# Forgetting attention: the reciprocal and scaling of a head behind the next head's minimum, and query, sample and memory steps held to places between the heads

## The chip, the cores and the metric

The kernel runs on 1 core of one Trainium2 chip. The metric is the device time of one execution in microseconds (us), the median over runs; lower is better. Engines are named as in the profile: PE is the matrix engine (PEld its weight loads), DVE the vector engine, ACT the scalar engine, POOL the general-purpose engine, SP the engine that issues most DMAs.

## The reference, cut to what matters

One inference step of a two-layer decoder trunk for a prompt of 512 tokens and 8 samples of 4 new tokens each, model width 1024. Layer 0 mixes state-space heads with sliding-window attention, layer 1 is the forgetting attention; each layer then has cross-attention into 256 memory tokens and a gated feed-forward network. The change lies in layer 1's mixer:

```python
def fox_attend(q, k, v, cum, q_off):
    '''Queries sit at key indices q_off..q_off+Tq-1; logit[t,s] += cum[t]-cum[s].'''
    ...
    bias = cq[..., :, None] - c[..., None, :]
    mask = jnp.arange(tk)[None, :] <= (q_off + jnp.arange(tq))[:, None]
    return gqa_attend(q, k, v, mask=mask, bias=bias)     # softmax(q k / 8 + bias) v

def fox_prompt(q, k, v, logf):                            # 4 blocks of 128 queries
    cum = jnp.cumsum(logf, axis=1)
    ...
    o = lax.map(lambda a: fox_attend(a[0], k, v, cum, a[1]), (qb, offs))

def mem_kv(mem, g, wk, wv):                               # the memory's keys and values, per layer
    mn = rms_norm(mem, g)
    return (mn @ wk)..., (mn @ wv)...
```

There are 16 query heads of 64 on 4 key heads. The samples attend in the same way to 1024 cached keys each, read page by page (128 keys a page) through a page table, and to their own 4 new ones.

## The kernel before

Everything is kept transposed: 128 features on the partitions, tokens along the free dimension. A float32 product is made of three faster ones, from a high and a low part of each factor, so each weight piece is loaded by SP, cast on ACT (L162) and its rest taken on DVE (L163) before PE uses it; `linear_steps` then yields after each output tile of 24 matmuls (8 of 128 inputs, three parts).

The order of work is settled when the program is built. Instructions are written in program order; a planner then fixes each engine's own order by estimated costs, taking among what is ready by its estimate that which was written first. So a piece of work written later can be planned ahead of a waiting one. `after` adds an edge that the planner obeys and that costs no wait on the chip. Tiles in the small accumulator memory (PSUM) have a tag each, and `psum` gives how many of a tag may be live: "tr" 3 (linear tiles), "sc" 2 (scores), "tp" 2 (transposes), "pv" 1 (values).

The forgetting attention (`odd`, from L1067) works on the prompt in 8 blocks, two halves `m` of the key heads by four blocks `c` of 128 queries, and each block has 8 heads (`fox_prompt`), 64 heads in all. A head of block `c` has W = 128 (c + 1) keys:

1. two score matmuls of W columns on PE (high part of the keys, then low part) into an "sc" tile (`bank`, L125);
2. on DVE the sum of scores and mask, its negative, and the smallest of that, in one instruction (L1183);
3. on ACT the exponential and the sum of it (L1184);
4. on DVE the reciprocal of the sum (L1185), and on POOL the scaling by it (L1186);
5. two heads later (`FOX_AHEAD`) `turn`: c + 1 transposes on PE (L141), copied by ACT or DVE in turn (L1166); after the block's last head the product with the values, copied out on DVE (L1173).

At the start of a block `fox_queries` (L1136) builds the block's high and low queries, 6 instructions on ACT and DVE. Between the heads the loop takes steps from three generators at the heads that `FOX_PLAN` (L40) lists: "q", the second half of the query projection (8 tiles); "s", the samples (`fox_sample`, L1243), in four groups of two samples, each with scores, softmax, transposes, and values, and with the loads of the next group's pages (32 DMAs of 128 KB on SP, L1260, keys then values); "m", the keys and values of layer 1's memory (`mem_begin`, `mem_k`, `mem_v`). Nothing but the planner's estimates keeps a step at its place.

After the loop the remaining heads are turned, the generators run out, the attention's output is split into parts (L246, L249) and multiplied by the output weights (`wo_d`), whose loads are held behind the copy of block 5's values (`whold`).

Of the kernel before, what the change touches and what calls it, by code (L numbers as in the profile page):

```python
# [14 lines left out]
AF = mybir.ActivationFunctionType  # L15
# [91 lines left out]
class Net:  # L107
    def __init__(self, nc, tc, ctx, I, O):
        self.nc, self.tc, self.ctx, self.I, self.O = nc, tc, ctx, I, O
        self.n = self.turn = 0  # L110
        self.hold = self.whold = self.last = None
# [25 lines left out]
    def mm(self, out, lhsT, rhs, start, stop):  # L137
        self.nc.tensor.matmul(out, lhsT, rhs, start=start, stop=stop)  # L138

    def tr(self, out, in_, k=P):  # L140
        self.nc.tensor.transpose(out, in_, self.ident[0:k, 0:k])  # L141
# [869 lines left out]
    def odd(self, st, nxt, fill):  # L1011
        nc, tc, I, O = self.nc, self.tc, self.I, self.O
        with ExitStack() as es:
# [53 lines left out]
            with tc.tile_pool(name="fox", bufs=1) as fx:  # L1067
                self.pvs = []
# [12 lines left out]
                self.banks = ['sc']  # L1081
# [28 lines left out]
    def fox_keys(self, kT, ncum):  # L1110
# [21 lines left out]
        self.zero(mask[:, 0:384])  # L1132
        self.after(nc.gpsimd.tensor_copy(mask[:, 384:512], self.cst[:, C_SWA + 128:C_SWA + 256]), self.last)
# [15 lines left out]
    def fox_prompt(self, q, K2, V, m, c, ahead):  # L1149
# [4 lines left out]
        Q = self.fox_queries(q, m, tok)  # L1154
# [19 lines left out]
        for r in range(2):  # L1174
            for i in range(4):
                sc = self.bank([P, 512])
                for z in range(2):
                    self.mm(sc[:, 0:W], Q[z][:, r, i], K2[z][:, m, r, 0:W], z == 0, z == 1)
# [6 lines left out]
                nc.vector.reciprocal(rec, den)  # L1185
                nc.gpsimd.tensor_scalar(pr[:, 0:W], pr[:, 0:W], rec, 1.0, ALU.mult, ALU.mult)  # L1186
                ahead.append((turn, pr, r, i))
                self.fox_turn(ahead, FOX_AHEAD)
                yield

# [52 lines left out]
    def fox_sample(self, q, kTs, Qb, ncs, V, lf, fx, S, sel):  # L1243
# [25 lines left out]
        self.sample_q(q, Qb)  # L1269
        for G in range(4):  # L1270
            sc = [self.psum("sc", [P, 4, 128]), self.psum("sc", [P, 4, 128])]
            sn = self.psum("tp", [P, 32])
            for u in range(2):
                self.mm(sc[u].rearrange("p a b -> p (a b)"), sel[:, 128 * (G % 2):128 * (G % 2) + 128], S[:, G // 2, 512 * u:512 * u + 512], True, False)
                for b2 in range(2):
                    for m in range(2):
                        a = 64 * b2 + 32 * m
                        lq = Qb[:, 2 * G + b2, m].rearrange("p r i t -> p (r i t)")
                        self.mm(sc[u][a:a + 32], lq, keys[G, b2][:, 4 * u:4 * u + 4, 128 * m:128 * m + 128], False, True)
# [7 lines left out]
            wk = self.prt[:, 2560:4736]  # L1287
            pr = wk[:, 0:1056]
# [4 lines left out]
            mx, nm, den, d1, rec = self.ty(3), self.ty(1), self.ty(3), self.ty(1), self.ty(1)  # L1293
            for u in range(2):
                nc.vector.tensor_reduce(mx[:, u:u + 1], sc[u].rearrange("p a b -> p (a b)"), AX.X, ALU.max)
            nc.vector.tensor_reduce(mx[:, 2:3], pr[:, 1024:1056], AX.X, ALU.max)
            nc.vector.tensor_reduce(nm, mx, AX.X, ALU.max, negate=True)
            for u in range(2):
                nc.scalar.activation(pr[:, 512 * u:512 * u + 512], sc[u].rearrange("p a b -> p (a b)"), AF.Exp, bias=nm, accum_out=den[:, u:u + 1])
            nc.scalar.activation(pr[:, 1024:1056], pr[:, 1024:1056], AF.Exp, bias=nm, accum_out=den[:, 2:3])  # L1300
            nc.vector.tensor_reduce(d1, den, AX.X, ALU.add)
            nc.vector.reciprocal(rec, d1)
# [17 lines left out]
            self.sample_o(q, Osb, G, 1)  # L1320
            if G < 3:
                load(vals, G + 1, "fox_v")
            yield


    def mem_begin(self, l):
# [12 lines left out]
        for k in range(KD):  # L1339
            g = self.par[:, G_MEM + 8 * l + k:G_MEM + 8 * l + k + 1]  # L1340
            self.split(mh, ml, raw[:, k], k, 0, 256, g)
            if first:
                self.square_acc(acc, raw[:, k], k, 256)
        if first:
            self.rstd(acc, self.mcol, self.mb, [(0, 0, 128), (1, 128, 128)])
# [381 lines left out]
    def run(self):  # L1727
# [5 lines left out]
        def memory(l):  # L1733
# [3 lines left out]
            m = self.mem_begin(l)  # L1737
# [129 lines left out]
```

## Time and profile before

| | |
|---|---|
| time, median of 3 runs | 1679.29 us (1678.39 to 1679.85) |
| the profiled execution's own time | 1679.51 us |
| its span in the profile | 1677.7 us |
| granted PE clock over the span | 0.993 |
| busy, share of the span | PE 97%, PEld 91%, DVE 71%, ACT 47%, POOL 20% |
| the fox stage's heads | 64, their minima from 992.9 us to 1157.8 us |

A row of a group reads: line, engine, operation, output<-inputs by the program's names, shape, count, then busy us, mean ns of one, then idle us of the engine just before them and what ended it. A row of the timeline reads: start in us, us taken, engine, line, operation, and in brackets the engine's idle time before it and what ended that. A row of a wait reads: who <- whom: us in total, times, longest. An SP row is the time to issue the DMAs, not to move the bytes. Matmuls are pipelined: a row's length is longer than the distance to the next.

### The profile page before, as it was taken

To read this page: it belongs to the slowest core of one execution; us is meant where nothing else is said; L and a number is where in the kernel's file an instruction comes from. 1 tells how busy PE (TensorE), PEld (TensorE's weight loads), DVE (VectorE), ACT (ScalarE), POOL (GpSimd) and SP (SyncE) were. 2 spreads that over 40 slices of the span, in tenths; PEclk is the share of its full clock that TensorE was granted. 3 is DMA by queue.
4 is the path that set the end of the run, shared out by engine and by line. 5 is a ranking of instruction groups with operands and counts; after the bars stand their busy time and mean duration, and the time that the engine had idled before them with its cause. 6 is when DMAs were issued, how large, how long until landed. Compare 5 with 4: busy or idle time off the path is not lost.

```text
span 1677.7 us, 32465 instructions
## 1 busy us (share of the span) xinstructions
PE 1627.3 (97%) x12720; PEld 1518.5 (91%) x12720; DVE 1196.5 (71%) x2322; ACT 795.1 (47%) x1637; POOL 333.5 (20%) x510
## 2 busy tenths in 40 slices
PE   6999999999999999999999998998999999999997
PEld 6999999868998999999999995656989999999997
DVE  6678789777777876767667577654667876767753
ACT  4367645344545444444445255544545444444434
POOL 6022323675422200000002103111313100000002
PEclk9999999999999999999999999999999999999999
DMA  5121243156442232323224433555451232323222
GB/s 187 55 64 52 86 154 126 37 192 217 156 138 91 94 113 83 107 77 114 82 70 135 141 118 110 165 170 186 132 183 52 86 125 85 109 86 102 76 72 83
DMA packets 71221, 189.27 MB, mean 113 GB/s; under 512 B 7612, under 2 KB 34012, under 8 KB 63452
## 3 DMA queue, kind: packets, MB, share of 16 engines
q1 hardware_dynamic: 69388, 184.84, 33.3%
q8 instruction: 100, 1.64, 0.4%
q10 hardware_dynamic: 1600, 1.83, 0.4%
q0 software_dynamic: 80, 0.52, 0.1%
q14 instruction: 53, 0.43, 0.1%
HBM read 172.22 MB, written 14.95 MB: 112 GB/s over the span
## 4 chain that ended last, share of the span: by engine, by line
PE 89%; DVE 4%; POOL 2%; issue 1%; DMA 1%; ACT 1%; DVEq 0%; SPq 0%; POOLq 0%; ACTq 0%
PE ps L138 64%; PE ps L1586 22%; PE ps L141 3%; POOL room L425 1%; DMA vr<-wd_v 0%; ACT prt L1184 0%; DMA o_s_ssm<-hb 0%; DVE meml L252 0%; DMA room<-wo_d 0%; DVE xs L902 0%; ACT split_t L162 0%; POOL sq L421 0%; DVE split_t L1567 0%; POOL E L862 0%; DVE prt L1183 0%
## 5 line engine op out<-in xcount | busy, mean ns | idle before, releaser
L138 PE MATMUL ps<-xh,split_t 128*128 128x288 f32 (+1 forms) x2304 | 463.9, 293 | 13.8 <-ACT split_t L162 11.8
L138 PEld LDWEIGHTS ps<-xh,split_t 128*128 128x128 f32 x2304 | 370.7, 190 | 17.0 <-ACT split_t L162 12.7
L1586 PE MATMUL ps<-xf,split_t 128*128 128x272 f32 x2592 | 348.9, 289 | 3.1 <-DVE split_t L1567 2.2
L138 PE MATMUL ps<-xl,split_t 128*128 128x256 f32 (+1 forms) x1152 | 338.5, 295 | 1.2 <-DVE xl L252 1.0
L1586 PEld LDWEIGHTS ps<-xf,split_t 128*128 128x128 f32 x2592 | 335.0, 188 | 4.4 <-DVE split_t L1567 3.1
L261 POOL TENSOR_TENSOR room<-room,sq 128x256 f32<-128x256 f32 (+1 forms) x96 | 87.4, 914 | 768.9 <-ACT sq L260 767.3
L138 PEld LDWEIGHTS ps<-xl,split_t 128*128 128x128 f32 x1152 | 218.5, 190 | 4.1 <-DVE xl L252 2.3
L138 PE MATMUL ps<-hh,fs 128*128 128x256 f32 (+1 forms) x1024 | 206.3, 288 | 0.0
L162 ACT CAST split_t<-room 128x1024 fp32r<-128x1024 f32 (+1 forms) x128 | 130.2, 1019 | 154.5 <-PE ps L138 112.2
L163 DVE TENSOR_TENSOR split_t<-room,split_t 128x1024 fp32r<-128x1024 f32 (+1 forms) x128 | 157.3, 1231 | 35.7 <-ACT split_t L162 35.1
L138 PEld LDWEIGHTS ps<-hh,fs 128*128 128x128 f32 x1024 | 164.9, 188 | 0.4 <-ACT fs L1630 0.4
L1567 DVE TENSOR_TENSOR split_t<-fr,split_t 128x1024 fp32r<-128x1024 f32 x108 | 131.7, 1220 | 36.6 <-ACT split_t L1566 36.4
L1566 ACT CAST split_t<-fr 128x1024 fp32r<-128x1024 f32 x108 | 113.4, 1052 | 90.5 <-PE ps L1586 54.7
L138 PE MATMUL ps<-hl,fs 128*128 128x256 f32 (+1 forms) x512 | 147.3, 288 | 0.0
L138 PE MATMUL ps<-oh,split_t 128*128 128x288 f32 (+1 forms) x512 | 107.2, 298 | 1.2 <-ACT oh L246 1.2
L138 PEld LDWEIGHTS ps<-hl,fs 128*128 128x128 f32 x512 | 96.4, 188 | 0.0
L138 PEld LDWEIGHTS ps<-oh,split_t 128*128 128x128 f32 x512 | 83.5, 192 | 6.1 <-ACT oh L246 3.0
L1630 ACT CAST fs<-room 128x512 fp32r<-128x512 f32 x64 | 39.4, 618 | 81.3 <-PE ps L138 67.2
L138 PE MATMUL ps<-ol,split_t 128*128 128x288 f32 (+1 forms) x256 | 76.1, 297 | 0.3 <-DVE ol L249 0.2
L252 DVE SCALAR_TENSOR_TENSOR xl<-x,room,xh 128x256 fp32r<-128x256 f32 (+1 forms) x96 | 69.7, 756 | 5.5 <-ACT xh L251 5.4
L138 PE MATMUL ps<-hh,split_t 128*128 128x256 f32 (+1 forms) x384 | 73.4, 288 | 0.0
L1643 DVE TENSOR_TENSOR x<-x,ps 128x256 f32<-128x256 f32 (+1 forms) x128 | 54.3, 433 | 25.7 <-PE ps L138 25.4
(426 smaller groups left out, 3118.7 us busy)
## 6 DMA issues: line engine op xcount, KB each, us to landing
fr<-wfi SPq DMA_DIRECT2D x36, 1024.0 KB
room<-wfo SPq DMA_DIRECT2D x64, 256.0 KB
room<-wo_e SPq DMA_DIRECT2D x16, 512.0 KB
xk<-mem_k SPq DMA_DIRECT2D x8, 1024.0 KB
xv<-mem_v SPq DMA_DIRECT2D x8, 1024.0 KB
room<-wfi SPq DMA_DIRECT2D x16, 512.0 KB
fox_k<-fox_k SPq DMA_DIRECT2D x64, 128.0 KB
fox_v<-fox_v SPq DMA_DIRECT2D x64, 128.0 KB
```

Of the source, the lines that this page charges most:

```text
L138: self.nc.tensor.matmul(out, lhsT, rhs, start=start, stop=stop)
L141: self.nc.tensor.transpose(out, in_, self.ident[0:k, 0:k])
L162: nc.scalar.copy(hi[:, 0:n], raw[:, 0:n])
L163: nc.vector.tensor_tensor(lo[:, 0:n], raw[:, 0:n], hi[:, 0:n].bitcast(F32), ALU.subtract)
L252: return nc.vector.scalar_tensor_tensor(ll, src, g, hh.bitcast(F32), ALU.mult, ALU.subtract)
L261: nc.gpsimd.tensor_tensor(acc, acc, sq[:, 0:N], ALU.add)
L425: nc.gpsimd.tensor_tensor(acc, acc, sq, ALU.add)
L1566: nc.scalar.copy(hi, t)
L1567: nc.vector.tensor_tensor(lo, t, hi.bitcast(F32), ALU.subtract)
L1586: self.nc.tensor.matmul(ps, w[a][:, k], x[:, b, k], start=start and k == 0 and i == 0, stop=k == 3 and i == 2, skip_group_check=True)
L1630: nc.scalar.copy(hi, raw)
L1643: nc.vector.tensor_tensor(x, x, ps, ALU.add)
```

## The change

It makes five edits, all in the fox stage but one.

- The reciprocal and the scaling of a head (`fox_scale`) are written after the next head's minimum and exponential; the last one after the loop.
- `mm` and `tr` give their instruction back, and `placed` sets an edge (`after`) from the first matmul or transpose of each step to the second score matmul of the head (`scored`) after which the step stands. The planner may no longer move a step's PE work ahead of that head. `FOX_PLAN` has other places: the query steps at heads 2 to 24, the samples' 17 steps at 25 to 58, the memory's 10 at 19 to 60, and two memory steps between the turns of the last heads.
- The next block's queries are built at the block's fourth head.
- A sample group takes its two score tiles one after the other, each finished by the minimum instruction (against a tile of zeros) that also copies it out; one exponential of 1056 columns takes the place of three; the group's last transpose and copies (`sample_o`) move behind the next yield. `mem_begin` of layer 1 yields after every second slice.
- The counts of "tr" and "sc" tiles become 4 and 3, in the whole kernel, and heads use two "sc" and one "tr" tile in turn from the start.

```diff
-for _a, _heads in (("q", range(4, 33, 4)), ("s", [33,34,36,38,40,41,43,45,47,49,51,53,55,57,59,61]), ("m", range(34, 64, 4))):
+for _a, _heads in (("q", (2, 4, 7, 10, 13, 16, 20, 24)), ("s", (25, 26, 28, 31, 33, 34, 36, 40, 41, 42, 44, 47, 49, 50, 52, 56, 58)), ("m", (19, 21, 23, 25, 35, 37, 39, 46, 54, 60))):
...
-        bufs = {"tr": 3, "sc": 2, "tp": 2, "pv": 1}[tag]
+        bufs = {"tr": 4, "sc": 3, "tp": 2, "pv": 1}[tag]
...
-        self.nc.tensor.matmul(out, lhsT, rhs, start=start, stop=stop)
+        return self.placed(self.nc.tensor.matmul(out, lhsT, rhs, start=start, stop=stop))
...
+    def placed(self, i):
+        if self.behind is not None:
+            self.behind, d = None, self.behind
+            self.after(i, d)
+        return i
...
-                self.banks = ['sc']
+                self.banks = ['sc', 'sc', 'tr']
...
-                for m in range(2):
-                    for c in range(4):
-                        for _ in self.fox_prompt(q, K2, V, m, c, ahead):
-                            heads += 1
-                            self.banks = ['sc'] if heads < 33 else ['sc', 'sc', 'tr']
-                            for a in FOX_PLAN.get(heads, ""):
-                                next(gens[a], None)
-                self.fox_turn(ahead, 0)
+                blocks = [(m, c) for m in range(2) for c in range(4)]
+                ready = lambda m, c: self.fox_queries(q, m, slice(128 * c, 128 * c + 128))
+                Q = ready(*blocks[0])
+                for j, (m, c) in enumerate(blocks):
+                    for _ in self.fox_prompt(Q, q, K2, V, m, c, ahead):
+                        heads += 1
+                        if heads % 8 == 4 and j < 7:
+                            nq = ready(*blocks[j + 1])
+                        for a in FOX_PLAN.get(heads, ""):
+                            self.behind = self.scored
+                            next(gens[a], None)
+                        self.behind = None
+                    Q = nq
+                self.fox_scale()
+                for _ in range(FOX_AHEAD):
+                    next(gens["m"], None)
+                    self.fox_turn(ahead, len(ahead) - 1)
...
-                nc.vector.reciprocal(rec, den)
-                nc.gpsimd.tensor_scalar(pr[:, 0:W], pr[:, 0:W], rec, 1.0, ALU.mult, ALU.mult)
+                self.fox_scale()
+                self.unscaled = pr[:, 0:W], rec, den
                 ahead.append((turn, pr, r, i))
                 self.fox_turn(ahead, FOX_AHEAD)
                 yield
+
+    def fox_scale(self):
+        if self.unscaled:
+            pr, rec, den = self.unscaled
+            self.nc.vector.reciprocal(rec, den)
+            self.nc.gpsimd.tensor_scalar(pr, pr, rec, 1.0, ALU.mult, ALU.mult)
+            self.unscaled = None
...
         for G in range(4):
-            sc = [self.psum("sc", [P, 4, 128]), self.psum("sc", [P, 4, 128])]
...
             for u in range(2):
+                sc = self.bank([P, 4, 128])
...
+                nc.vector.tensor_tensor_reduce(pr[:, 512 * u:512 * u + 512], sf, self.zeros.to_broadcast([P, 512]), -1.0, 1e30, ALU.add, ALU.min, mx[:, u:u + 1])
+                if u == 0:
+                    yield
...
-            gate = nc.vector.tensor_tensor(pr[:, 1024:1056], sn, c[:, C_MN + 32 * G:C_MN + 32 * G + 32], ALU.add)
+            gate = nc.vector.tensor_tensor_reduce(pr[:, 1024:1056], sn, c[:, C_MN + 32 * G:C_MN + 32 * G + 32], -1.0, 1e30, ALU.add, ALU.min, mx[:, 2:3])
             if G < 3:
                 load(keys, G + 1, "fox_k")
-            yield
-            ...
-            for u in range(2):
-                nc.scalar.activation(pr[:, 512 * u:512 * u + 512], sc[u].rearrange("p a b -> p (a b)"), AF.Exp, bias=nm, accum_out=den[:, u:u + 1])
-            nc.scalar.activation(pr[:, 1024:1056], pr[:, 1024:1056], AF.Exp, bias=nm, accum_out=den[:, 2:3])
+            nc.vector.tensor_reduce(nm, mx, AX.X, ALU.min)
+            nc.scalar.activation(pr, pr, AF.Exp, bias=nm, scale=-1.0, accum_out=den)
...
-            self.sample_o(q, Osb, G, 1)
             if G < 3:
                 load(vals, G + 1, "fox_v")
             yield
+            self.sample_o(q, Osb, G, 1)
```

More of the change, by code (lines that the diff above doesn't have):

```diff
@@ L110, in __init__ @@
         self.n = self.turn = 0
-        self.hold = self.whold = self.last = None
+        self.hold = self.whold = self.last = self.behind = None
         pool = lambda name, **k: ctx.enter_context(tc.tile_pool(name=name, bufs=1, **k))
@@ L1132, in fox_keys @@
         self.zero(mask[:, 0:384])
+        self.zeros = mask[:, 0:1]
         self.after(nc.gpsimd.tensor_copy(mask[:, 384:512], self.cst[:, C_SWA + 128:C_SWA + 256]), self.last)
@@ L1147, in fox_queries, with fox_prompt @@
         return Q
-    def fox_prompt(self, q, K2, V, m, c, ahead):
+    def fox_prompt(self, Q, q, K2, V, m, c, ahead):
         nc = self.nc
@@ L1269, in fox_sample @@
         self.sample_q(q, Qb)
+        yield
         for G in range(4):
-            sc = [self.psum("sc", [P, 4, 128]), self.psum("sc", [P, 4, 128])]
             sn = self.psum("tp", [P, 32])
+            wk = self.prt[:, 2560:4736]
+            pr = wk[:, 0:1056]
+            mx = self.ty(3)
             for u in range(2):
-                self.mm(sc[u].rearrange("p a b -> p (a b)"), sel[:, 128 * (G % 2):128 * (G % 2) + 128], S[:, G // 2, 512 * u:512 * u + 512], True, False)
+                sc = self.bank([P, 4, 128])
+                sf = sc.rearrange("p a b -> p (a b)")
+                self.mm(sf, sel[:, 128 * (G % 2):128 * (G % 2) + 128], S[:, G // 2, 512 * u:512 * u + 512], True, False)
                 for b2 in range(2):
@@ L1278, in fox_sample @@
                         lq = Qb[:, 2 * G + b2, m].rearrange("p r i t -> p (r i t)")
-                        self.mm(sc[u][a:a + 32], lq, keys[G, b2][:, 4 * u:4 * u + 4, 128 * m:128 * m + 128], False, True)
+                        self.mm(sc[a:a + 32], lq, keys[G, b2][:, 4 * u:4 * u + 4, 128 * m:128 * m + 128], False, True)
+                nc.vector.tensor_tensor_reduce(pr[:, 512 * u:512 * u + 512], sf, self.zeros.to_broadcast([P, 512]), -1.0, 1e30, ALU.add, ALU.min, mx[:, u:u + 1])
+                if u == 0:
+                    yield
             for b2 in range(2):
@@ L1286, in fox_sample @@
                 self.mm(sn[a:a + 64], ncs.rearrange("p h t -> p (h t)"), self.ident[0:32, 0:32], False, True)
-            wk = self.prt[:, 2560:4736]
-            pr = wk[:, 0:1056]
-            gate = nc.vector.tensor_tensor(pr[:, 1024:1056], sn, c[:, C_MN + 32 * G:C_MN + 32 * G + 32], ALU.add)
+            gate = nc.vector.tensor_tensor_reduce(pr[:, 1024:1056], sn, c[:, C_MN + 32 * G:C_MN + 32 * G + 32], -1.0, 1e30, ALU.add, ALU.min, mx[:, 2:3])
             if G < 3:
                 load(keys, G + 1, "fox_k")
-            yield
-            mx, nm, den, d1, rec = self.ty(3), self.ty(1), self.ty(3), self.ty(1), self.ty(1)
-            for u in range(2):
[L1295 to L1299, printed above, removed]
-            nc.scalar.activation(pr[:, 1024:1056], pr[:, 1024:1056], AF.Exp, bias=nm, accum_out=den[:, 2:3])
-            nc.vector.tensor_reduce(d1, den, AX.X, ALU.add)
-            nc.vector.reciprocal(rec, d1)
+            nm, den, rec = self.ty(1), self.ty(1), self.ty(1)
+            nc.vector.tensor_reduce(nm, mx, AX.X, ALU.min)
+            nc.scalar.activation(pr, pr, AF.Exp, bias=nm, scale=-1.0, accum_out=den)
+            nc.vector.reciprocal(rec, den)
             yield
@@ L1343, in mem_begin @@
                 self.square_acc(acc, raw[:, k], k, 256)
+            elif k % 2:
+                yield
         if first:
@@ L1736, in memory @@
             nc.gpsimd.memset(t[:, 0:1], 0.0)
-            m = self.mem_begin(l)
+            m = yield from self.mem_begin(l)
             yield from self.mem_k(l, m, self.mk)
```

7 lines of the change are left out of this document (3 added, 4 removed).

## The prediction

> **What bounds the kernel now.** I read the page first (engines, forty slices), then stretches of the fox stage, then its groups by shape, its waits and its timeline.
>
> ```profile
> span 1677.7 us, 32465 instructions
> PE 1627.3 (97%) x12720; PEld 1518.5 (91%) x12720; DVE 1196.5 (71%) x2322; ACT 795.1 (47%) x1637; POOL 333.5 (20%) x510
> PEld 6999999868998999999999995656989999999997
> ```
>
> The matrix engine is the bound, but a matmul's row is longer than the time it keeps the next one waiting, so PE at 97% hides losses. The weight loads (PEld) show them: slices 25 to 28, 42 us each, fall to 5 or 6 tenths. That is the forgetting attention, 990 to 1165 us, the one stage that this change edits. Stretches of it, and a dense one after it (stretch, length, then busy us and count of PE, PEld, DVE, ACT, POOL, then granted clock, DMA share, GB/s):
>
> ```profile
> 990.00:995.00 5.00, 5.00 (x43) 5.00 (x42) 4.15 (x12) 1.73 (x5) 0.38 (x1) 1.00 0.30 78
> 1000.00:1005.00 5.00, 5.00 (x43) 4.81 (x43) 4.55 (x16) 3.43 (x10) 1.13 (x4) 1.00 0.62 187
> 1030.00:1035.00 5.00, 4.25 (x20) 2.27 (x18) 3.67 (x14) 3.72 (x11) 1.77 (x3) 1.00 0.02 3
> 1100.00:1105.00 5.00, 5.00 (x21) 2.79 (x21) 0.55 (x1) 0.37 (x1) 0.00 (x0) 1.00 0.65 192
> 1145.00:1150.00 5.00, 1.37 (x14) 0.80 (x7) 0.92 (x1) 1.99 (x5) 0.22 (x1) 0.81 0.62 233
> 1150.00:1155.00 5.00, 4.38 (x20) 4.15 (x21) 4.88 (x19) 3.55 (x11) 1.39 (x2) 0.51 0.38 108
> 1175.00:1180.00 5.00, 5.00 (x42) 5.00 (x41) 4.66 (x8) 3.63 (x9) 2.51 (x3) 1.00 0.87 357
> 990.00:1047.00 57.00, 52.07 (x325) 39.33 (x323) 43.95 (x146) 32.57 (x92) 17.23 (x36) 1.00 0.45 139
> 1047.00:1165.00 118.00, 109.38 (x880) 72.43 (x879) 66.99 (x225) 59.19 (x164) 19.03 (x35) 0.97 0.52 154
> ```
>
> A dense stretch does 42 matmuls of 256 or 288 columns in 5 us, 0.119 us each, or 21 of 512 columns, 0.238 each. While query projections ran beside the heads (990, 1000) PE did 43 in 5 us. At 1030, with the projections used up, it did 20, mostly small. The stage's PE work, priced so, from groups of 990 to 1165 (shapes, count, busy us, mean ns) and from runs of back-to-back rows:
>
> ```profile
> L141 PE MATMUL ps<-room,prt 128*128 128x128 f32 x192 | 32.8, 280 | 2.4 <-POOL prt L1186 0.9 <-DVE q L582 0.4 <-ACT prt L1299 0.4
> L138 PE MATMUL ps<-PT,odd 128*64 128x512 f32 x72 | 25.5, 608 | 0.5 <-ACT PT L1166 0.5
> L138 PE MATMUL ps<-fox_k,odd 128*32 128x512 f32 x64 | 13.5, 604 | 0.0
> L138 PE MATMUL ps<-fox_v,prt 128*32 128x128 f32 x256 | 9.0, 275 | 0.0
> L138 PE MATMUL ps<-split_t,memh 128*128 128x512 f32 x32 | 10.9, 402 | 0.5 <-ACT prt L1311 0.5
> L138 PE MATMUL ps<-split_t,meml 128*128 128x512 f32 x16 | 6.3, 393 | 0.0
> L138 PE MATMUL ps<-kh,qst 128*128 128x512 f32 x16 | 7.8, 488 | 2.2 <-DVE ty L1183 2.2
> L138 PE MATMUL ps<-kl,qst 128*128 128x512 f32 x16 | 6.3, 395 | 0.0
> ...
> 1042.28 0.44 PE ps L141 x4
> ...
> 1038.10 1.94 PE L138 MATMUL ps<-PT,odd 128*64 128x512 f32 x8
> ...
> 1142.60 1.74 PE L138 MATMUL ps<-fox_v,prt 128*32 128x128 f32 x56
> ```
>
> Transposes 192 x 0.11 (0.44 for four) = 21; probabilities times values 72 x 0.24 (1.94 for eight) = 17.5; cached keys 13.5 by their busy time; cached values 256 x 0.031 (1.74 for 56) = 8; 80 of 512 columns x 0.238 = 19; the other 541 of the 1205 (325 and 880 above), mostly of 256 and 288 columns, x 0.119 = 64. Sum 143 us of the stage's 175: **32 us are lost**. DVE's 111 us (43.95 and 66.99) fit beside that, and ACT's 92. Where the loss sits, first a head of 384 keys, then the waits that end in it (weight loads, then DVE):
>
> ```profile
> 1028.71 0.54 DVE L1183 CUSTOM_DVE_ANT_0 prt<-ps,prt 128x384 f32<-128x384 f32 x1
> ...
> 1029.29 0.62 ACT L1184 ACTIVATE prt<-prt,ty 128x384 f32<-128x384 f32 x1 [0.69 <-DVE ty L1183]
> 1029.81 0.18 ACT L1184 ACTIVATION_READ_ACCUMULATOR prt<-prt,ty 128x1 f32 x1
> ...
> 1030.03 0.16 DVE L1185 RECIPROCAL ty<-ty 128x1 f32<-128x1 f32 x1 [0.24 <-ACT prt L1184]
> 1030.11 0.54 DVE L1183 CUSTOM_DVE_ANT_0 prt<-ps,prt 128x384 f32<-128x384 f32 x1
> ...
> PEld ps L138 <- DVE ty L1183: 9.8, 16, 0.9
> ...
> L1185 DVE RECIPROCAL ty<-ty 128x1 f32<-128x1 f32 x64 | 10.3, 161 | 20.2 <-ACT prt L1184 19.5
> ...
> ACT split_t L162 <- DMA room<-wo_d: 3.8, 1, 3.8
> ...
> 1141.80 0.85 SPq L158 DMA_DIRECT2D room<-wo_d  x2
> ```
>
> The minimum (L1183), the exponential (L1184) and the reciprocal (L1185) make a ring: DVE runs in order, so the next minimum waits behind a reciprocal that waits for ACT. 1028.71 to 1030.11 is 1.40 us a head, of which DVE works 0.78. The last two rows are the end: an output weight asked for at 1141.80 is late, its cast stands at the head of ACT's queue with a head's exponential behind it, and PE drops to 1.37 of 5 us.
>
> **The change part by part.**
>
> *Reciprocal and scaling behind the next minimum.* No instruction more or less. Removed from the ring: ACT's 0.62 + 0.18 and two hand-overs; DVE then does the next minimum in that time. The gain is bounded by the 20.2 us that DVE idled before L1185 and by 0. I take 8: nearest is the 9.8 us that PE's weight loads stood behind L1183, less a little, because the next limit, DVE's own work, lies close (4.55 of 5 us at 1000). Scaling on POOL comes a head later, so a head's transposes have one head in hand instead of two. POOL is busy 1.77 of 5 us, so this costs nothing unless heads run faster than a scaling and two hand-overs. **-8.**
>
> *Steps held between the heads.* A step's first matmul may no longer be planned ahead of the score that it is held behind. Moved: eight query steps (24 matmuls each; per two steps one weight load on SP, a 1 us cast on ACT, a 1.2 us subtraction on DVE, two evacuations) from a bunch before 1020 to heads 2 to 24; the four sample groups from heads 33-61 to 25-58, with one score bank at a time and a step more; the memory's scaling to heads 19-25, its products to 35-60 and the tail. The casts, subtractions and loads carry no edge and may still run early. The same PE work is thus beside heads that now have none. The 32 us less 9.8 (ring) and 6.6 (end, below) leave 15.6 that this could fill; bounds 0 and 15.6. Half, because heads 1 to 24 already overlapped with all the query work and lose some of it: **-8.**
>
> *Next block's queries at every fourth head.* ACT and DVE casts move earlier by four heads; same count. Their cover is the loop itself; at worst they delay a minimum by one subtraction per block. **0.**
>
> *Sample softmax.* Per group, two reductions of 512 columns and a few tiny ones give way to two minima that also copy, and three exponentials with their read-outs to one:
>
> ```profile
> L1295 DVE TENSOR_REDUCE ty<-ps 128x1 f32<-128x512 f32 x8 | 5.5, 689 | 2.9 <-PE ps L138 2.8
> ...
> L1183 DVE CUSTOM_DVE_ANT_0 prt<-ps,prt 128x512 f32<-128x512 f32 x16 | 10.8, 673 | 0.0
> ...
> L1299 ACT ACTIVATE prt<-ps,ty 128x512 f32<-128x512 f32 x8 | 5.4, 683 | 5.7 <-DVE ty L1297 5.7
> ```
>
> DVE 0.689 against 0.673 a piece: even. ACT saves about one read-out pair per group, under 1 us, beside other work. The score banks are free after the minimum, not after the exponential. **0.**
>
> *Page loads, SP's queue.* Each group's 32 loads hang on the group before; SP issues them in order with all weights behind. Moved past them: two memory weights and the output weights.
>
> ```profile
> 1055.73 8.70 SPq L1260 DMA_DIRECT2D fox_k<-fox_k  x16
> ...
> 1071.75 8.24 SPq L1260 DMA_DIRECT2D fox_v<-fox_v  x16
> ...
> 1085.36 15.72 SPq L1260 DMA_DIRECT2D fox_k<-fox_k  x16
> ```
>
> One group is at best 8.70 + 8.24 = 17 us of SP, and 30 us apart now (1055.73, 1085.36). The plan gives a group eight heads with their fill, 16 to 18 us by the prices above: close to SP's floor. PE would wait in order at a group's first score. Bounds 0 and 3 x 8 (15.72 against 8); I take **+2.**
>
> *The end.* 3.6 us of idle PE (1.37 of 5) and 20 matmuls at a granted clock of 0.51, which at full clock need some 2.4 us less: 6 to 6.6 in all. The last group's values are asked for four heads earlier, so the output weight's load stands less far behind. Bounds 0 and 6.6; **-2**, since nothing in the change orders that load.
>
> The Trainium skill, "TensorE: Matmul & The Clock Gate", Part 1, says that an idle window of about 3.4 us halves the array's clock. The trace agrees: 3.6 idle, then 0.51. By that rule the half-speed part goes entirely or not at all, which would make this term -6 or 0 and the total 1659 or 1665.
>
> *Buffers.* The cap of live "tr" tiles goes from 3 to 4, of "sc" from 2 to 3, everywhere in the kernel. In the fox stage this lets scores run a head further ahead, within the terms above. Elsewhere PE is near full (slices at 9); **0**, with the loss as a rival.
>
> Sum -8 -8 +2 -2 = **-16**. The profiled execution took 1679.51 us (span 1677.7), 0.2 above the median 1679.29; so about **1663 us**.
>
> **The rivals.**
> (a) *The sample chain keeps its pace.* If the groups stay about 30 us apart because their pages come no faster, only the earlier start pays: the first group's scores move from after head 33 to heads 26-28, some 8 us by the ring's 1.4 us a head. Gives 1671. For: 15.72 us for one load of keys. Against: DMA's share at 1030 is 0.02, so there is room to spread.
> (b) *All of it is filled.* The stage runs throughout as at 990 to 1005, 43 matmuls in 5 us beside heads; most of the 32 us go: 1650. Against: DVE at 4.15 to 4.55 of 5 there, and longer heads need more.
> (c) *It does not do what it says.* The planner's order differs little in effect, since work held back is missing earlier: heads 1 to 24 lose what later ones win. 1676 to 1682.
> (d) *Slower: the caps.* They now add up to 4 + 3 + 2 + 1 = 10 tiles, where the old ones were 8. If eight is all that fits, a linear tile can hold the place that a chain's tile needs, for its 24 matmuls, 24 x 0.119 = 2.9 us. Place: the state-space stage, where weight loads are already thin:
>
> ```profile
> 300.00:400.00 100.00, 93.95 (x693) 77.26 (x690) 75.25 (x139) 44.15 (x98) 74.86 (x82) 0.98 0.38 130
> ```
>
> Six such waits (16 us / 2.9) eat the gain; ten make it 1692. For: nothing else there is edited to avoid it. Against: the old caps allowed eight at once and its chain rarely waits for anything but its own engines.
> The Trainium skill, "PSUM — Partial Sum Buffer", Specifications, gives eight banks of 2 KiB per partition, so ten full tiles cannot live at once; no row before the change shows it. By that rule alone (d) would be possible, not certain.
>
> **How the numbers follow.** Forecast -16, within 1655 to 1668: 0.47. (a) 0.20. (b) 0.12. (c) 0.10, of which 0.06 lies within 0.2% (3.4 us, what a measurement here can tell from no change), 0.04 just faster. (d) 0.11. Faster: 0.47 + 0.20 + 0.12 + 0.04 = 0.83; same 0.06; slower 0.11. The range leaves out (d), half of (c) and the far end of (b): from 1647 (all 32 us) to 1679.
>
> **What would show it.** Ring: spacing of L1183 at 384 keys falls from 1.40 to about 1.2 us, and DVE's idle time before the reciprocal from 20 to under 5. Hold: 17 to 20 matmuls in 5 us at 1020 to 1045 become 25 or more, and query projections appear among the heads of 384 keys. Samples: key loads 18 to 22 us apart. End: no 5 us slice with the clock near 0.5. The prediction is wrong if PE waits for page loads, if DVE is full while PE is not, or if stages before 960 us take longer than they do now, which would be (d).

## The result and the profile after

| | before | after |
|---|---|---|
| time, median of 20 runs of each | 1676.67 us | 1681.09 us |
| lowest to highest | 1672.14 to 1682.03 | 1678.03 to 1684.49 |
| ratio after / before | | 1.0027, 95% interval 1.0018 to 1.0035 |
| the profiled execution, its span | 1679.51, 1677.7 | 1678.73, 1677.0 |

The change makes the kernel slower, by 0.27% or some 4.5 us. The profiled execution of after is one of the shorter of its 20 runs, and that of before lies 2.8 us over its median, so the two traces are equally long. They show where work moved; the 4.5 us themselves come from the timed runs and can't be found in the traces. In the traces the heads start 4.0 us earlier in after (988.95 for 992.95) and the stage ends 1.1 us earlier. The page of after, engines and weight loads in forty slices:

```profile
span 1677.0 us, 32458 instructions
PE 1629.7 (97%) x12720; PEld 1522.6 (91%) x12720; DVE 1195.6 (71%) x2326; ACT 793.2 (47%) x1621; POOL 333.1 (20%) x510
PEld 7999999868998999999999996556989999999997
```

The dip is where it was, slices 25 to 28, and as deep. Stretches of after, then the same two of before (columns as in the prediction):

```profile
985.00:1045.00 60.00, 58.21 (x387) 45.13 (x388) 49.27 (x161) 35.89 (x97) 15.38 (x33) 1.00 0.47 141
1045.00:1165.00 120.00, 107.88 (x837) 71.74 (x838) 62.45 (x220) 54.08 (x144) 21.62 (x37) 0.93 0.48 146
1020.00:1045.00 25.00, 23.43 (x138) 13.78 (x134) 20.78 (x64) 15.23 (x40) 7.40 (x15) 1.00 0.41 126
```

```profile
985.00:1045.00 60.00, 55.22 (x357) 43.42 (x355) 46.84 (x149) 34.62 (x94) 16.59 (x35) 1.00 0.41 124
1045.00:1165.00 120.00, 111.24 (x886) 73.34 (x887) 68.89 (x230) 60.51 (x168) 19.67 (x36) 0.97 0.52 155
```

In the first 60 us PE does 30 matmuls more and is busy 3.0 us more; in the next 120 it does 49 fewer, is busy 3.4 us less, and its mean clock falls from 0.97 to 0.93. What the first half won, the second gave back. The clock is lost in three places of the stage, where before had one; stretches of 5 us of after:

```profile
1075.00:1080.00 5.00, 5.00 (x30) 4.75 (x31) 3.00 (x15) 4.32 (x15) 2.16 (x6) 0.70 0.48 135
1095.00:1100.00 5.00, 3.56 (x10) 2.97 (x11) 2.64 (x16) 3.35 (x12) 1.87 (x4) 0.51 0.88 237
1135.00:1140.00 5.00, 5.00 (x16) 2.83 (x15) 2.02 (x8) 1.72 (x5) 1.32 (x3) 0.55 0.53 214
```

The second half is read best from DVE, around the last sample group. DVE's timeline of after (L1199 a head's minimum, L1211 its reciprocal, L1310 and L1320 the sample group's minima, L1326 its reciprocal):

```profile
1105.14 0.54 DVE L1199 CUSTOM_DVE_ANT_0 prt<-ps,prt 128x384 f32<-128x384 f32 x1
...
1119.21 0.69 DVE L1310 CUSTOM_DVE_ANT_0 prt<-ps,prt 128x512 f32<-128x512 f32 x1 [0.70 <-PE ps L138]
...
1127.05 0.69 DVE L1310 CUSTOM_DVE_ANT_0 prt<-ps,prt 128x512 f32<-128x512 f32 x1 [0.24 <-PE ps L138]
...
1130.29 0.16 DVE L1326 RECIPROCAL ty<-ty 128x1 f32<-128x1 f32 x1 [1.33 <-ACT prt L1325]
1130.37 0.54 DVE L1199 CUSTOM_DVE_ANT_0 prt<-ps,prt 128x384 f32<-128x384 f32 x1
```

Head 52's minimum is at 1105.14 and head 53's at 1130.37, 0.08 us after the sample's reciprocal. For 25.2 us no head moves. All four groups end so: the next head's minimum starts 0.08 us behind L1326, and the stretch without a head around it is 8.8, 17.5, 14.1 and 25.2 us. The same block is in before (8.6, 12.0, 5.6 and 13.2 us, around its L1302). DVE's timeline of before, around its last group:

```profile
1127.62 0.67 DVE L1183 CUSTOM_DVE_ANT_0 prt<-ps,prt 128x512 f32<-128x512 f32 x1
...
1140.77 0.16 DVE L1302 RECIPROCAL ty<-ty 128x1 f32<-128x1 f32 x1
1140.85 0.67 DVE L1183 CUSTOM_DVE_ANT_0 prt<-ps,prt 128x512 f32<-128x512 f32 x1
```

PE's timeline of after shows that the heads' scores were ready (head 53's second score matmul is the first row) and that PE then starved:

```profile
1127.68 0.34 PE L138 MATMUL ps<-kl,qst 128*128 128x384 f32 x1
1130.97 0.50 PE L138 MATMUL ps<-kh,qst 128*128 128x512 f32 x1 [2.96 <-DVE ty L1199]
```

And SP, which brings the sample groups' keys and values page by page:

```profile
1058.96 9.09 SPq L1284 DMA_DIRECT2D fox_v<-fox_v  x16
1068.10 0.33 SPq L1279 DMA_DIRECT2D tab<-pages  x1
1073.00 15.49 SPq L1284 DMA_DIRECT2D fox_k<-fox_k  x16
1088.75 8.71 SPq L1284 DMA_DIRECT2D fox_v<-fox_v  x16
...
1098.32 0.29 SPq L1279 DMA_DIRECT2D tab<-pages  x1
...
1103.78 15.62 SPq L1284 DMA_DIRECT2D fox_k<-fox_k  x16
1119.50 0.85 SPq L165 DMA_DIRECT2D room<-wo_d  x2
```

From 1059 to 1119 SP has hardly a gap: values 9 us, the page numbers' load and the wait for it 5, keys 15.5. A group takes some 30 us (1073.00 to 1103.78), as in before (28 and 30). So two things stand out, a block of heads behind each sample softmax and SP's queue, and the experiments begin with them.

### The profile page after: what moved, and what is told of

Its sections match the earlier page's. It is cut to its first block, busy times and chain, and to the rows that moved or that the text cites. A ratio compares the mean times of both kernels' runs of the same rounds, so it can differ in the third digit from the quotient of the medians.

```text
span 1677.0 us, 32458 instructions
## 1 busy us (share of the span) xinstructions
PE 1629.7 (97%) x12720; PEld 1522.6 (91%) x12720; DVE 1195.6 (71%) x2326; ACT 793.2 (47%) x1621; POOL 333.1 (20%) x510
## 4 chain that ended last, share of the span: by engine, by line
PE 89%; DVE 4%; POOL 2%; issue 2%; SPq 1%; ACT 1%; DMA 1%; DVEq 0%; POOLq 0%; ACTq 0%
PE ps L138 64%; PE ps L1612 22%; PE ps L141 3%; SPq L1284 1%; POOL room L432 1%; DVE meml L259 0%; SPq L1280 0%; DMA o_s_ssm<-hb 0%; DVE xs L909 0%; POOL sq L428 0%; DVE split_t L1593 0%; POOL E L869 0%; DVE x L1779 0%; ACT split_t L169 0%; DMA x<-x 0%
## 5 line engine op out<-in xcount | busy, mean ns | idle before, releaser
L169 ACT CAST split_t<-room 128x1024 fp32r<-128x1024 f32 (+1 forms) x128 | 130.3, 1020 | 155.8 <-PE ps L138 106.3
```

The costliest lines, as they stand in the source:

```text
L169: nc.scalar.copy(hi[:, 0:n], raw[:, 0:n])
```

## The experiments

Each ran in five rounds beside the kernel before, on one chip; the chip is not the same for all of them, so ratios are compared and not times. "From after" is the difference of the two ratios times 1676.7 us; two ratios whose intervals overlap are not told apart. "Stage" is, in the profiled execution, the time from the first head's minimum (988.95 in after) to the last product of probabilities with values (its 12 last matmuls start at 1163.50 in after, the last at 1166.1). "Heads left" is the number of heads whose minimum comes after the last sample group's reciprocal.

| label | kernel | us | ratio to before (95%) | from after | stage us | heads left |
|---|---|---|---|---|---|---|
| | before | 1676.67 | 1 | -4.5 | 174.2 | 7 |
| | after | 1681.09 | 1.0027 (1.0018-1.0035) | 0 | 177.1 | 12 |
| e1 | after, own tiles | 1679.64 | 1.0021 (1.0011-1.0032) | -1.0 | 177.2 | 5 |
| e2 | before, own tiles | 1713.55 | 1.0218 (1.0202-1.0234) | | 185.9 | |
| e3 | after, no putting off | 1686.71 | 1.0064 (1.0048-1.0080) | +6.2 | 182.7 | 12 |
| e4 | before, putting off | 1676.87 | 1.0002 (0.9993-1.0012) | | 173.1 | |
| e5 | after, pages once | 1672.44 | 0.9969 (0.9958-0.9980) | -9.7 | 168.4 | 12 |
| e6 | after, pages once, own tiles | 1663.50 | 0.9920 (0.9904-0.9937) | -17.9 | 161.8 | 9 |
| e7 | e6, groups 2-4 with group 1's pages | 1664.68 | 0.9921 (0.9907-0.9935) | -17.8 | 161.0 | |
| e8 | before, pages once | 1670.75 | 0.9955 (0.9941-0.9968) | | 165.5 | 7 |
| e9 | after, counts 3 and 2 | 1705.87 | 1.0175 (1.0159-1.0192) | +24.8 | 177.4 | |
| e10 | after, no edges | 1684.18 | 1.0044 (1.0028-1.0060) | +2.9 | 180.4 | |
| e11 | e6, no putting off | 1669.19 | 0.9958 (0.9944-0.9973) | -11.6 | 166.9 | |
| e12 | e6, no edges | 1666.26 | 0.9938 (0.9923-0.9952) | -14.9 | 162.2 | |
| e13 | after, groups 2-4 later | 1675.10 | 0.9995 (0.9984-1.0006) | -5.4 | 170.8 | 7 |
| e14 | e8, putting off | 1669.37 | 0.9960 (0.9947-0.9974) | | 164.8 | |
| e15 | before, all limits lifted, putting off | 1667.84 | 0.9950 (0.9936-0.9965) | | 163.9 | |
| e16 | before, own tiles, counts 4 and 3 | 1671.20 | 0.9967 (0.9956-0.9979) | | 166.7 | 2 |
| e17 | e6, groups 2-4 later | 1662.15 | 0.9903 (0.9885-0.9920) | -20.8 | 159.9 | 2 |
| e18 | after, all groups later | 1674.14 | 0.9989 (0.9979-0.9999) | -6.4 | 171.6 | 7 |

In the expectations, "PE's loss" is worked out as in the prediction: for each matmul, the time to the next one's start less its price. Between 1000 and 1160 us it is 37.5 us in before, 38.7 in after, 38.3 in e1 and 25.0 in e6.

### The block of heads: e1, e2, e16

```diff
-            nm, den, rec = self.ty(1), self.ty(1), self.ty(1)     # the sample group's
+            nm, den, rec = (fx.tile([P, 1], F32, tag=f"sy{i}", bufs=2, name=self.nm("sy")) for i in range(3))
```

> The changed kernel with one edit: the three one-column tiles of a sample group's softmax (minimum, denominator, reciprocal) come from buffers of their own instead of the ring that the heads take theirs from. Theory T (a head behind a sample's softmax can't be planned until that softmax has given its tiles back, so its minimum stands behind the sample's reciprocal): heads' minima stand ahead of the sample's reciprocals, the three stretches without any head (17.5, 14.1 and 25.2 us) fall below 10 us, PE loses under 24 us instead of 39 between 1000 and 1160 us, and the time falls by 10 to 18 us to 1663 to 1671. Rival K (the key loads, some 30 us apart, set the groups' pace): the stretches close but PE's loss moves elsewhere and the time stays within 3 us of the changed kernel. Rival B (the two raised PSUM counts cost time in other stages): no more than 3 us gained, and stages before 960 us as before.

The block went: a head's minimum now comes 0.6 to 4.0 us ahead of each sample reciprocal, and the longest stretch without a head is 11.9 us. The time hardly moved (-1.0 us). PE's loss stayed, as rival K has it (38.3 us): the chain of work now waits for the last group's keys, and then for output weights. Parts of the chain of e1, near the stage's end:

```profile
1100.81 2.54 DMA tab<-pages
...
1117.65 1.92 DMA fox_k<-fox_k
...
1132.10 7.08 DMA room<-wo_d
```

Between the first and the second row SP alternates page-number reads (L1280) and key loads (L1284); the third is an output weight that SP asked for late, with ACT waiting on it. So T's mechanism was right (sharing the ring of tiles puts the heads behind the softmax) and its price wrong: a second limit lay directly underneath. How the planner comes to that order wasn't seen. For a ring of 12 tiles instead of 6 the planner's order (an order alone, without a time) still has the next head directly behind each sample reciprocal, so it is the sharing and not the number of tiles.

> The kernel before with the same one edit. T: the same block is there before (a head's minimum at 1082.56 directly behind the sample's reciprocal), so its stretches of 12 to 14 us without a head shrink below 9 and the time falls by 4 to 10 us to 1667 to 1673; the 20 us of DVE's wait ahead of the heads' reciprocals stay. K: within 3 us of before.

This one said little about the stage. Its matmuls per 100 us fell far from the edit too. Stretches of e2, then of e9 (below), then of before:

```profile
0.00:100.00 100.00, 83.56 (x609) 80.89 (x610) 65.29 (x129) 41.51 (x88) 28.73 (x46) 0.97 0.33 112
1300.00:1400.00 100.00, 94.06 (x717) 91.86 (x718) 78.00 (x114) 46.88 (x78) 19.27 (x22) 0.98 0.28 95
```

```profile
0.00:100.00 100.00, 84.11 (x609) 80.84 (x610) 64.83 (x129) 41.52 (x88) 28.16 (x46) 0.95 0.34 112
1300.00:1400.00 100.00, 94.06 (x720) 91.89 (x719) 75.03 (x107) 44.44 (x71) 14.26 (x18) 0.98 0.26 88
```

```profile
0.00:100.00 100.00, 86.58 (x640) 83.42 (x641) 68.68 (x138) 45.50 (x98) 32.84 (x50) 0.98 0.33 113
1300.00:1400.00 100.00, 97.42 (x768) 96.54 (x767) 81.65 (x115) 45.85 (x72) 7.14 (x8) 1.00 0.30 102
```

609 matmuls against 640, 717 against 768. Of the kernels run here, these two alone have from the planner a slower order for the whole program; in its order for PE the fourth output tile of the very first projection begins at the 82nd matmul, in every other kernel here at the 28th. Both have counts of 3 and 2. Before, e4, e8 and e14 have them too and are not slowed, so the counts alone don't bring that order; what tips it stays open.

> The kernel before with own tiles for the sample softmax and PSUM counts of 4 and 3. If the 1713 us with own tiles alone came from a plan with less PSUM for the whole program: the 25 us lost outside the stage are gone, 1670 to 1677. If the own tiles themselves cost on the kernel before: over 1690.

With counts of 4 and 3 beside the own tiles the cost outside the stage is gone: 1671.20 us, 0.33% under before. So e2 was slow by the old counts and the new tiles together, through the order of the whole program, and lifting the block helps the kernel before too (the counts alone were not tried there).

### SP's queue: e5, e6, e7, e8

```diff
-                tab = fx.tile([1, 16], I32, tag="tab", bufs=2, name=self.nm("tab"))
-                self.after(nc.sync.dma_start(tab, I["pages"][:, 16 * G:16 * G + 16]), kd)
-                page[G] = [nc.sync.value_load(tab[0:1, x:x + 1], ...) for x in range(16)]
+                if G == 0:
+                    page["t"] = fx.tile([1, 64], I32, tag="tab", bufs=1, name=self.nm("tab"))
+                    self.after(nc.sync.dma_start(page["t"], I["pages"][:, 0:64]), kd)
+                page[G] = [nc.sync.value_load(page["t"][0:1, 16 * G + x:16 * G + x + 1], ...) for x in range(16)]
```

> The changed kernel with one edit: the page numbers of all four sample groups come in one small load at the first group, not one of 16 numbers ahead of each group's keys; SP still reads each number into a register. Rival K (SP's queue sets the pace from the second group on: keys, values and the wait for the page numbers follow each other without a gap, some 30 us a group): three waits of 5 us ahead of the keys go, the last group's keys are issued some 10 to 15 us earlier (from 1104 to about 1092), and the time falls by 6 to 14 us to 1667 to 1675. Theory T (the heads' ring alone): the stretches without a head stay, the time stays within 3 us of 1681.

9.7 us gained, with the block of heads left standing (stretches of 8.6, 16.8, 10.9 and 11.2 us). SP's timeline of e5:

```profile
1072.70 8.20 SPq L1285 DMA_DIRECT2D fox_k<-fox_k  x16
...
1094.75 8.47 SPq L1285 DMA_DIRECT2D fox_k<-fox_k  x16
```

Not only the waits of 5 us went: the issue of 16 key loads fell from 15.5 us to 8.2, since the register reads no longer stand between them, and a group takes 22 us.

> The changed kernel with both edits, tiles of their own for the sample softmax and the page numbers loaded once. If each is a bound that hides the other (K and T together): PE loses under 22 us between 1000 and 1160 us where the changed kernel loses 39, and the time is 1658 to 1666. K alone: as with the page numbers alone, within 3 us. Neither: within 3 us of 1681.

Together they are worth 17.9 us where alone they gave 1.0 and 9.7: each hid part of the other. PE's loss fell to 25.0 us, not quite under the 22 expected. PE's stretches of e6, where after had 58.21 and 107.88:

```profile
985.00:1045.00 60.00, 57.47 (x379) 44.15 (x379) 50.31 (x163) 36.02 (x99) 17.30 (x35) 1.00 0.40 118
1045.00:1165.00 120.00, 117.41 (x953) 83.18 (x951) 71.41 (x238) 61.69 (x162) 23.74 (x39) 0.99 0.65 208
```

```diff
+                if G == 0:                       # the load and the 16 reads, for the first group alone
+                    ...
+                page[G] = page[0]
```

> As the kernel with both edits, but groups two to four read the pages of the first group, so that SP reads no further page numbers: 48 register reads and three small loads are left out (samples 2 to 7 attend to other samples' pages). It bounds what SP's part can be worth. K: keys are issued in 8 to 9 us a group, as the values are, instead of 15.6; the time is 2 to 6 us under that with the page numbers loaded once, near 1655 to 1662. If the two are equal within 2 us, the register reads aren't on the path once the small loads are gone.

This kernel leaves out the page numbers of three groups, and is equal to e6 within the intervals: once the page numbers are there early, reading them costs nothing on the path.

> The kernel before with the page numbers loaded once and nothing else. K: its SP queue has the same solid stretch from 1071 to 1142 us with two waits of 4 to 5 us, so the time falls by 5 to 12 us to 1664 to 1671. T: within 3 us of before.

7.5 us off the kernel before by the ratio, so SP's queue bounded that kernel too. The two kernels with pages loaded once stand at 0.9955 and 0.9969: the change still gains nothing while the block stands.

### The parts of the change: e3, e4, e9, e10, e11, e12

> The changed kernel with the reciprocal and the scaling back directly behind their own head's exponential; places, queries and buffers as changed. If the putting off is a gain that something else cancels (T): DVE's wait ahead of the heads' reciprocals returns to 15 to 20 us, the stretches without heads stay at 14 to 25 us, and the time rises by 3 to 8 us to 1684 to 1689. If the putting off is itself what costs (rival P: the head ahead of a sample's softmax is scaled a head later, behind the stretch): the time falls by 3 to 8 us to 1673 to 1678.

```diff
-                self.fox_scale()
                 self.unscaled = pr[:, 0:W], rec, den
+                self.fox_scale()
```

Putting off is a gain in the changed kernel, 6.2 us. Waits (who <- whom: us in total, times, longest), first of DVE in e3, then of DVE and ACT in after:

```profile
DVE ty L1210 <- ACT prt L1200: 22.0, 35, 1.2
```

```profile
DVE ty L1211 <- ACT prt L1200: 5.2, 11, 1.2
...
ACT split_t L169 <- DMA room<-wo_d: 5.2, 2, 4.9
```

The ring's wait is 22.0 us without the putting off and 5.2 with it. The second row, ACT's wait for an output weight, belongs to the end of the stage, taken up below.

```diff
-                nc.vector.reciprocal(rec, den)                        # on the kernel before
-                nc.gpsimd.tensor_scalar(pr[:, 0:W], pr[:, 0:W], rec, 1.0, ALU.mult, ALU.mult)
+                self.fox_scale()
+                self.unscaled = pr[:, 0:W], rec, den
```

> The kernel before with only the reciprocal and the scaling put off behind the next head's minimum; places, queries, sample softmax and buffers as before. T: DVE's wait ahead of the reciprocals falls from 20 to about 5 us, and as the changed kernel's first half showed some 5 us less PE loss, the time is 3 to 8 us under before, 1669 to 1674. P: 0 to 5 us over before, since the last head ahead of each sample softmax is now scaled behind it.

Neither theory. On the kernel before the idle time ahead of the reciprocals falls from 20.2 us to 1.6, and the time does not move:

```profile
L1195 DVE RECIPROCAL ty<-ty 128x1 f32<-128x1 f32 x64 | 9.9, 156 | 1.6 <-ACT prt L1185 1.4
```

Head 33 comes 4.7 us earlier (1045.0 for 1049.7), the stage ends 0.7 us earlier.

```diff
-        bufs = {"tr": 4, "sc": 3, "tp": 2, "pv": 1}[tag]
+        bufs = {"tr": 3, "sc": 2, "tp": 2, "pv": 1}[tag]
```

> The changed kernel with the PSUM counts back at 3 and 2 (changed: 4 and 3). If the counts are what costs the changed kernel its gain (rival B, the prediction's case of a slower kernel, 1692): the time falls by 3 to 10 us to 1671 to 1678 and stages outside 985 to 1165 us lose less. If they are neutral, as the prediction took them: 1681 within 3 us.

24.8 us slower, and none of it in the stage (177.4 us against 177.1). It is the slower order of the whole program shown above. Raising the counts was cover that the other edits need, not a cost.

```diff
-                            self.behind = self.scored
```

> The changed kernel without the added edge that lets the first PE instruction of a step start only behind the score of its head; the places of the steps stay. The prediction took holding and spreading the steps as worth 8 us: by that the time rises by 4 to 8 us to 1685 to 1689. If SP's queue and the heads' ring set the pace (K and T together), the edge only moves work within the same stretches: 1681 within 3 us.

Without the edges the time is 2.9 us longer, between the two expectations, but the intervals of e10 and after overlap, so a gain from the edges is not shown.

e11 and e12 make the edits of e3 and e10 on e6.

> The kernel with both edits (page numbers once, own tiles for the sample softmax, 1663.5), with the reciprocal and the scaling back directly behind their own head's exponential. The prediction gave the putting off 8 us (0 to 20): with the two other limits away it should show whole, 1669 to 1676. If the putting off is worth only what it gave in the changed kernel, 5.6 us: 1667 to 1671. If it is worth nothing, as on the kernel before: 1663 within 3 us.

With both limits lifted the putting off is worth 6.4 us (0.9958 against 0.9920), as much as in the changed kernel and not more.

> The kernel with both edits, without the added edges. If the edges are worth something once nothing else sets the pace: 1667 to 1672 (4 to 8 us slower than 1663.5). If only the places count: 1663 within 3 us. If the edges hold work back that could fill PE: 1657 to 1661.

3.0 us longer, but again the intervals overlap (0.9923 to 0.9952 and 0.9904 to 0.9937); the stage is equal, 162.2 and 161.8 us.

### The places: e13, e18, e17, and the rest: e14, e15

```diff
-("s", (25, 26, 28, 31, 33, 34, 36, 40, 41, 42, 44, 47, 49, 50, 52, 56, 58))
+("s", (25, 26, 28, 31, 33, 36, 41, 43, 45, 46, 49, 51, 53, 55, 57, 59, 61))
```

> The changed kernel with only the places of the sample steps of groups two to four moved to later heads, about where the kernel before has them (softmax behind heads 41, 49 and 57 instead of 36, 44 and 52). If the early places cost (keys come no sooner, since SP's queue brings a group every 30 us, so that more heads stand behind the softmax when they come: 12 heads after the last one instead of 7): the last heads are fewer behind the last softmax and the time falls by 5 to 10 us to 1671 to 1676. If the form of the sample steps costs, or the places don't matter: 1681 within 3 us.

5.4 us back. DVE's timeline of e13, around the last sample reciprocal:

```profile
1117.16 0.69 DVE L1199 CUSTOM_DVE_ANT_0 prt<-ps,prt 128x512 f32<-128x512 f32 x1 [1.69 <-POOL prt L1212]
...
1136.60 0.17 DVE L1326 RECIPROCAL ty<-ty 128x1 f32<-128x1 f32 x1 [1.40 <-ACT prt L1325]
1136.68 0.67 DVE L1199 CUSTOM_DVE_ANT_0 prt<-ps,prt 128x512 f32<-128x512 f32 x1
```

The block is still there, and the reciprocal comes later than in after (1136.60 for 1130.29), and yet the stage is 6 us shorter: 7 heads and not 12 stand behind it.

```diff
-("s", (25, 26, 28, 31, 33, 34, 36, 40, 41, 42, 44, 47, 49, 50, 52, 56, 58))
+("s", (32, 33, 34, 36, 38, 40, 41, 43, 45, 47, 49, 51, 53, 55, 57, 59, 61))
```

> The changed kernel with all sample steps at about the heads where the kernel before has them (first group's softmax behind head 34, then 41, 49, 57). If the first group's early place costs as the others do: 1666 to 1671. If the rest of the cost lies in the form of the steps or in the queries and memory steps: 1675 within 3 us, as with only groups two to four late. If the first group's early place gains: 1678 to 1683.

The first group's place makes no difference that shows (0.9989 against 0.9995).

e17 is e6 with the places of e13; e14 and e15 join edits already shown, as the table says.

> The kernel with both edits (1663.5 us), with the sample steps of groups two to four at the later heads. If the early places cost only because heads wait behind a softmax whose keys SP brings late, they now gain or are neutral: later places give 1663 to 1668. If the early places cost in any case: later places give 1657 to 1661.

With both limits lifted later places are 2.9 us faster where they were 5.4 faster before, and the intervals overlap. This fits early places that cost mainly through the two limits; that they cost nothing in themselves is not shown. At 1662.15 us this is, with e6, the fastest kernel here, 0.97% under before (0.9885 to 0.9920).

> The kernel before with the putting off and the page numbers loaded once. Alone, the first gave nothing and the second 6 us (1670.75). If SP's queue hid the first: 1664 to 1668. If the putting off is worth nothing with the places of before, whatever SP does: 1671 within 2 us.

0.9960 against 0.9955 without the putting off: still nothing. SP's queue alone is not what hides it on the kernel before. What does was not found.

> The kernel before with the putting off, the page numbers loaded once, own tiles for the sample softmax, and PSUM counts of 4 and 3; its places, its form of the sample steps and its queries. Against 1663.5 us of the changed kernel with the same limits lifted, this is the worth of the places, the edges, the queries and the sample form together. If they cost: under 1661. If they gain, as the prediction took it (8 us for holding and spreading): 1667 to 1672. If nothing: 1663 within 2 us.

0.9950 against e6's 0.9920: with the limits away, the change's places, edges, queries and sample form together gain some 5 us (the intervals just touch). Lifting the limits takes 17.9 us off after and some 8 off before (e15, with the putting off), and this is what turns the change from slower to faster.

## Why the prediction was wrong

Forecast 1663, range to 1679, slower at 0.11; measured 1681.09. Point by point:

- **Putting off, -8.** Held, a little oversized: 6.2 us in the changed kernel, 6.4 with the limits lifted. DVE's idle time fell from 20.2 to 5.2 us, nearly as foretold (under 5); the spacing at 384 keys cannot be compared, since query projections now run between those heads. The prediction did not see that the gain depends on the rest: nothing on the kernel before.
- **Steps held, -8: the step that failed, in sign.** What was to show it came in the first half: 138 matmuls in the 25 us from 1020, 27.6 per 5 us where 17 to 20 had been. But the 15.6 us left over were taken as room that work could fill, without asking what kept the work away. The edges gain 2.9 us at best, inside the noise; the sample steps' earlier places, which the term took for part of its gain, cost 5.4 to 6.4.
- **Page loads, +2: the mis-sized term under it.** The prediction took a group's floor from the second group, 8.70 + 8.24 = 17 us, and called the pace near it. The third group needs 15.5 + 8.7 us and 5 for the page numbers, some 29 us, and that is the pace of before and after; with the page numbers loaded once (e5) it falls to 22. The 15.72 stood in the prediction, priced as 3 x 8 us of possible delay instead of as the pace itself.
- **Rival (a)** named this pace, but took the earlier start as a gain of 8 us. With the keys' time fixed by SP, an earlier place only puts more heads behind the softmax that waits for them (12 for 7).
- **Rival (c)**, 1676 to 1682, has the measured time in its range, but by luck: it let heads 1 to 24 lose what later ones win, and here the first half won and the second lost.
- **Sample softmax, 0.** The cost of its instructions was right. What was missed is that the heads behind it cannot pass it; no rival had this, though before shows it (5.6 to 13.2 us without a head around L1302).
- **Buffers, 0, and rival (d).** The loss at the raised counts did not come: stages outside are unchanged, and it is without them that 24.8 us are lost.
- **The end, -2.** Not gained: ACT waits 5.2 us for an output weight, 3.8 before, and there are three half-clock stretches for one. The reading "3.6 idle, then 0.51" was not exact either: in before PE is idle from 1146.4 to 1150.6, and the clock is down from 1148.1, 1.7 us into that wait.

The sum by the runs: -6.2 (putting off), -2.9 (edges) and +5.4 to 6.4 (places) come to about -3, where +4.5 was measured, so some 7 to 8 us have no cause of their own here, if the parts add (each is known to 2 or 3 us). What was not undone singly is the form of the sample steps, the queries at the fourth head, the memory steps. The clock may be part of it: its mean over the runs is 0.988 in after and 0.992 to 0.993 in before, which over 1681 us is at most some 7 us; but e1 has 0.992 and gains only 1.0 us, so this is not shown. With the limits lifted these, with places and edges, gain some 5 us (e15 against e6), so they too may lengthen the block or SP's queue; that is argued, not shown. That e6 reaches the predicted 1663 us is no support for the sum: it took two edits that the change lacks.

## What to carry to other kernels

Idle time beside a stage is room only if what the work waits for can come sooner: find the supplier's pace (here one queue's 30 us a group) before pricing a move to earlier places. When a step that waits for data shares a ring of tiles with a running loop, a planner like this one may stop the loop at it, as here; give it tiles of its own, and lift the supplier's limit with it, for each alone may show little of what the two give together (here 1.0 and 9.7 of 17.9 us). And when one edit slows stages that it doesn't touch, compare matmul counts per stretch far from it first, or the run will be read as evidence on the edit.

## What the runs showed of the hardware

PE's clock halves without a long wait. In after, the last matmuls ahead of the third group's burst end in the stretch from 1094, and the next starts at 1096.44, 1.87 us of idle time later. Stretches of 1 us:

```profile
1094.00:1095.00 1.00, 0.57 (x3) 0.25 (x2) 0.49 (x2) 0.41 (x1) 0.00 (x0) 1.00 0.44 138
1095.00:1096.00 1.00, 0.00 (x0) 0.00 (x0) 0.11 (x2) 0.86 (x2) 0.00 (x0) 0.55 0.85 221
1096.00:1097.00 1.00, 0.56 (x2) 0.56 (x3) 0.79 (x6) 0.58 (x3) 0.35 (x1) 0.50 0.88 246
...
1100.00:1101.00 1.00, 1.00 (x5) 0.70 (x4) 0.00 (x1) 0.67 (x2) 0.53 (x2) 0.50 1.02 381
1101.00:1102.00 1.00, 1.00 (x7) 1.00 (x6) 0.68 (x2) 0.00 (x0) 0.00 (x0) 0.54 0.80 315
```

The clock is down by 1095.1, when PE has been idle for about half a microsecond, so the wait of 1.87 us is not by itself what brought it down. It stays at 0.50 until 1101.9, with PE full from 1097. A burst of heads thus pays twice, for the wait and for some 5 us of work at half speed. The 3.41 us ahead of the fall, then the half-clock stretch:

```profile
1091.69:1095.10 3.41, 2.68 (x21) 1.54 (x19) 1.50 (x7) 0.88 (x2) 0.00 (x0) 1.00 0.73 214
1095.10:1101.92 6.82, 5.48 (x18) 4.59 (x18) 3.24 (x18) 3.92 (x13) 2.40 (x5) 0.50 0.89 270
```

In after the falls come at 23.31, 374.89, 412.43, 1074.62, 1095.10 and 1132.65 us, each a whole number of 3.41 us behind the first (103, 114, 308, 314 and 325), and up to there the clock stays down for 3.41 or 6.83 us. In every other trace here the falls lie on such a grid too. So it looks as if the clock were settled anew every 3.41 us, by the work of the stretch just past. The Trainium skill, "TensorE: Matmul & The Clock Gate", Part 1, lets the half-rate state begin "after ≥1 idle window (~3.4µs)". This trace agrees on the length, but its stretch ahead of the fall was not idle: 21 matmuls, mostly small, with PE busy for 2.68 of 3.41 us. The measurement decides: a sparse stretch was enough, and the length of the longest wait in it does not tell. e6 loses the clock at 1074.65 beside a wait of 1.33 us, and e16 keeps it throughout the stage with one of 1.46. How sparse is too sparse was not tried.

The other surprise is the price of reading an address just ahead of using it: 16 loads took SP 15.5 us with a register read between them and 8.2 with the reads done early. The reads themselves don't get cheaper (16 in a row took 9.1 us from 1030.87 in after, 0.57 us each); done early they are off the path: e7, which leaves most of them out, is no faster than e6.
